# Second layer of a two-stream feed forward: one moving operand of 512 columns in place of two of 256

## The chip, the core and the metric

The kernel runs on one core of a Trainium2 chip. The metric is the device time of one execution in microseconds (us). A core has TensorE (PE, matrix products; PEld are its weight loads), VectorE (DVE), ScalarE (ACT), GpSimd (POOL) and SyncE (SP, which here issues the DMAs). Each engine runs its own instructions in order and waits for the others through semaphores.

## The reference, cut to what matters

The program is a whole small network. Its first block has two layers, and works on two streams of 256 tokens each, `x` (called a below) and `ctx` (called b), both 1024 wide. The second stream ends in the second layer's mixer.

```python
D_MODEL = 1024; SEQ = 256; CTX_LEN = 256; DEPTH = 2; D_FF = 2816
def swiglu(h, w_gate_up, w_down):
    gate, up = jnp.split(h @ w_gate_up, 2, axis=-1)
    return (jax.nn.silu(gate) * up) @ w_down
def sandwich_ffn(x, w_gate_up, w_down, g_pre, g_post, shift, scale, gate):
    h = modulate(rms_norm(x, g_pre), shift, scale)
    return x + 0.5 * gate * rms_norm(swiglu(h, w_gate_up, w_down), g_post)
for l in range(DEPTH):
    x = sandwich_ffn(x, w_ffn_gate_up[l, 0], w_ffn_down[l, 0], ...)
    ctx = sandwich_ffn(ctx, w_ffn_gate_up[l, 0], w_ffn_down[l, 0], ...)
    ... # mixer of both streams
    x = sandwich_ffn(x, w_ffn_gate_up[l, 1], w_ffn_down[l, 1], ...)
    if not last:
        ctx = sandwich_ffn(ctx, w_ffn_gate_up[l, 1], w_ffn_down[l, 1], ...)
```

So three feed forwards of the program have two streams and share their weights between them: layer 0's first and second, and layer 1's first. The change touches `@ w_down` in these three. A second block follows (attention, an mLSTM and two feed forwards of the one stream), which the change does not touch.

## The kernel before

Features lie on the 128 partitions and tokens on the free axis. Every float32 operand of a product is split into a high and a low float32r part, and one term of a product is three matmuls into the same bank of PSUM: high weights by high data, high by low, low by high. ACT makes the high part of a piece of weights (`whi`, L93, 128x1024, eight blocks of 128x128), DVE the low part (`wlo`, L95), from `raw` that SP loads. Six pieces are held at a time (`RING`), three raw ones (`RAW`).

`ffn_two` is the feed forward of two streams. It goes through the hidden width of 2816 in two halves of 11 blocks (`HF`). In each half, for each of the 11 hidden blocks, PE makes the gate and the up product of stream a and then of stream b (`gu`, 258 columns), and `gu_evac` turns each pair into the high and low part of the hidden block: `tg`, `tu` and `af` on DVE, `sl` and `ah` (L250) on ACT, `al` (L251) on DVE. The hidden blocks are kept for each stream apart, in `aha`, `ala`, `ahb`, `alb`.

Then comes the second layer, called "down" here: 8 output blocks of 128 features (`KD`), for each stream, each a sum over the half's 11 hidden blocks. `blocks` issues three matmuls of 256 columns for each term (L597 to L599, tile `ps_dn`), with the depth outermost; output blocks 0 and 1 go on together. `lagged` sets the order of streams and blocks: stream a's blocks 0 and 1, stream b's 0 and 1, then block 2 of a, block 2 of b, and so on. In the second half of the width the last four blocks (`LAG`) are all of a's and then all of b's, so that a's norm can begin while b's blocks run. In the first half ACT copies a finished block out of PSUM (L668); in the second half DVE adds it to that copy (L671), ACT squares it and DVE sums the squares, for the norm behind it (`post`).

PE runs in the order in which the code is written. The order of DVE and ACT is made by the framework's scheduler, with priorities. Beside the products, DVE and the DMA queue work off the modulation vectors: for each of 128 rows `mod_chunk` loads 128x1024 (`wm`) and DVE multiplies it with the conditioning vector (L502). These rows are spread over the three feed forwards by a table (`mods`), some before each down block of stream a.

```python
o = [(a, (0, 1)), (b, (0, 1))]
for d in range(2, KD - lag):
    o += [(a, (d,)), (b, (d,))]
return o + [(a, (d,)) for d in range(KD - lag, KD)] + [(b, (d,)) for d in range(KD - lag, KD)]
```

Of the kernel before, what the change touches and what calls it, by code (L numbers as in the profile page):

```python
# [18 lines left out]
P = 128  # L19
T = 256  # L20
# [17 lines left out]
# columns of the packed parameter array  # L38
# [10 lines left out]
# columns of the packed constants  # L49
# [16 lines left out]
class Stream:  # L66
    """One set of 256 tokens, features on partitions."""


class Weights:  # L70
    """Weights in the order in which they are used: loaded ahead, and split into two float32r parts."""
# [27 lines left out]
    def queued(self):  # L99
        """Long instructions are not to come between the short ones of a norm's chain."""  # L100
        return self.tc.issue_after(self.behind) if self.behind is not None else nullcontext()
# [14 lines left out]
class Chunks:  # L116
    """Weights that come as a row of [128, 128] blocks, eight to a piece."""
# [14 lines left out]
class Kernel:  # L132
    """TensorE runs its instructions in the order written here. Work that waits for other engines is
    held in chains, whose steps are put between the matrix products of the main line."""
# [6 lines left out]
    # ---------------------------------------------------------------- plan of the weights  # L141
# [53 lines left out]
    # ---------------------------------------------------------------- chains  # L195
# [22 lines left out]
    def later(self, c, gap, fn, label=None, after=0):  # L218
        """fn as the next step of a chain: gap terms behind the step before it, after terms from now."""
        c.append([gap, fn, label, self.now + after])  # L220
# [7 lines left out]
    # ---------------------------------------------------------------- small helpers  # L228
# [16 lines left out]
    def split(self, hi, lo, src, scale=None):  # L245
        """hi + lo = src * scale, both float32r."""
# [11 lines left out]
    def mm3(self, out, terms, main=False):  # L258
        """out = sum over terms of (whi + wlo).T @ (xhi + xlo); the product of the low parts is below float32."""
# [9 lines left out]
    def gemm(self, outs, ws, s, n):  # L269
        """Blocks of a product of s's tokens; several blocks go on together, one part of the depth at a time."""  # L270
# [10 lines left out]
    # ---------------------------------------------------------------- norms  # L281
    def rsqrt_v(self, y, v, t):
        """y = v ** -0.5 by Newton's iteration."""
# [10 lines left out]
    def stat(self, s, acc):  # L294
        """s.rt[token] = rsqrt(mean of the squares + eps), tokens on partitions."""
# [14 lines left out]
    def spread(self, s):  # L310
        """s.rt with tokens on the free axis, the same on all partitions."""
# [36 lines left out]
    def begin(self):  # L348
        """The first two modulation vectors, the first norm of both streams, and the first products."""
# [66 lines left out]
    def post(self, s, g5, y, nxt, wait):  # L416
        """x += g5 * rms_norm(y), then the next norm's input: nxt = (factors, shift). y: one tile, or a list
        of blocks."""
# [40 lines left out]
    def residual(self, s, d, ps, nxt, acc):  # L459
        """One block of a product back into the stream, and the next norm's input."""  # L460
# [12 lines left out]
    # ---------------------------------------------------------------- modulation vectors  # L473
    def load_cond(self, pool):
        """silu of the two conditioning vectors, the same on all partitions."""
# [14 lines left out]
    def mod_chunk(self, l, c):  # L490
        """128 entries of a modulation vector, for both streams."""
# [25 lines left out]
    def both(self, l, c):  # L517
        """The second stream ends in the last mixer."""
        return l == 0 or c < 5 * KD

    def mod_done(self, l, vec):
        """Once a vector is there: the factors that norms and residuals take from it."""
# [14 lines left out]
    # ---------------------------------------------------------------- feed forward  # L537
# [16 lines left out]
    def times_r(self, s, t, ps):  # L554
        """Two blocks times r; they lie in one bank of PSUM or in two."""
# [30 lines left out]
    def blocks(self, s, ds, w, n, tag, ready=None):  # L586
        """Blocks ds of a product of depth n * 128, the depth outermost; ready: called before each part."""
# [14 lines left out]

    def lagged(self, streams, lag):
        """Blocks of the last product: the first stream ends some blocks before the second."""
        a, b = streams
        o = [(a, (0, 1)), (b, (0, 1))]
        for d in range(2, KD - lag):
            o += [(a, (d,)), (b, (d,))]
        return o + [(a, (d,)) for d in range(KD - lag, KD)] + [(b, (d,)) for d in range(KD - lag, KD)]

    def ffn_start(self, key, s, n, side=1):
        """The first two products, before the phase's own buffers are there: `side` of them go on together, as
        far as the norm has come."""
# [12 lines left out]
    def ffn_two(self, l, i, first, nxts, start):  # L626
        """Feed forward of two streams, in two halves of the hidden width."""
# [5 lines left out]
        with ExitStack() as es:  # L633
            self.fp = pool = es.enter_context(self.tc.tile_pool(name="ffn", bufs=1))
            for s in self.pair:
                s.ah = pool.tile([P, HF, T], F32R, name="ah" + s.name)
                s.al = pool.tile([P, HF, T], F32R, name="al" + s.name)
# [5 lines left out]
            for h in range(2):  # L643
# [17 lines left out]
                for s, ds in self.lagged(self.pair, LAG if h else 0):  # L661
                    if s is sa:
                        for d in ds:
                            self.mod_chunks(mods.get(KF + h * KD + d, ()))
                    for d, ps in self.blocks(s, ds, lambda d, c: w(HF * d + c), HF, "ps_dn"):
                        y = s.y[:, d, :]
                        if h == 0:
                            nc.scalar.activation(out=y, in_=ps, func=AF.Copy)  # L668
                            continue
# [1053 lines left out]
```

## Time and profile before

| what | value |
|---|---|
| time, median of 3 runs | 2641.85 us (2633.56 to 2644.76) |
| the profiled execution, span from first to last instruction | 2634.0 us |
| PE busy | 2520.9 us, 96% of the span |
| DVE busy | 1858.6 us, 71% |
| ACT busy | 1172.5 us, 45% |
| the six down stretches, from first to last matmul | 59.7, 60.6, 59.7, 60.6, 63.9, 60.6 us |
| matmuls of 256 columns in these | 3168, in six groups of 528 |

For the profiled execution the profile gives only the span; it lies inside the range of the runs, 7.85 us under their median. A busy share counts overlapping instructions once. PE's matmuls are pipelined: a matmul of 256 columns is shown as 0.28 us long, but the next one starts 0.11 us after it, so the pace is read from starts, not from durations. PEclk is the granted clock of TensorE, as a share of 2.4 GHz: 1.00 is 2.4 GHz and 0.50 is 1.2 GHz.

### The profile page before, as it was taken

The numbers are of one execution on the slowest core, as the hardware profiler recorded it, in microseconds if no ns is written. First come the engines' busy times: TensorE is split into PE (matmuls) and PEld (weight loads), VectorE is DVE, ScalarE is ACT, GpSimd is POOL, SyncE is SP. The second block draws the span as 40 slices with busy tenths as digits, with TensorE's granted clock in tenths as the row PEclk, the third lists the DMA queues.
The fourth block names the chain that finished last, engine by engine and source line by source line (L and its number), as shares of the span: only waits on it lengthen the run. The fifth ranks groups of instructions, "written<-read, shape, count | busy, mean of one in ns | idle before, by whom it ended". The sixth has DMA issues, their size and how long they took to land. (4 is left out here: it accounts for less than half of the span.)

```text
span 2634.0 us, 49868 instructions
## 1 busy us (share of the span) xinstructions
PE 2520.9 (96%) x20335; PEld 2445.3 (93%) x20335; DVE 1858.6 (71%) x3734; ACT 1172.5 (45%) x2062; POOL 74.3 (3%) x131
## 2 busy tenths in 40 slices
PE   7999998999999999999999888998999999999998
PEld 5999997889999999999998778998999999978998
DVE  5998548676998546984547767757877676666764
ACT  4332324664432333332334555545555554565442
POOL 0000001210000000000000310000000000000000
PEclk9999998999999999999999989999999999998999
DMA  8666323622566321674232734554444465533553
GB/s 300 206 209 208 106 89 72 80 45 74 183 206 220 104 91 63 221 252 159 97 97 75 88 73 152 194 186 134 152 145 145 133 204 184 168 110 109 189 176 120
DMA packets 105254, 383.17 MB, mean 145 GB/s; under 512 B 13560, under 2 KB 13688, under 8 KB 103360
## 3 DMA queue, kind: packets, MB, share of 16 engines
q1 hardware_dynamic: 101984, 370.89, 42.5%
q0 software_dynamic: 3040, 9.09, 4.3%
q8 instruction: 159, 2.61, 0.4%
q14 instruction: 71, 0.58, 0.1%
HBM read 378.88 MB, written 1.05 MB: 144 GB/s over the span
## 5 line engine op out<-in xcount | busy, mean ns | idle before, releaser
L93 ACT ACTIVATE whi<-raw 128x1024 fp32r<-128x1024 f32 x559 | 588.6, 1055 | 570.9 <-PE gu L277 186.0
L95 DVE TENSOR_TENSOR wlo<-raw,whi 128x1024 fp32r<-128x1024 f32 x559 | 680.4, 1219 | 217.8 <-ACT whi L93 215.7
L278 PE MATMUL gu<-hha,wlo 128*128 128x258 f32 (+1 forms) x2112 | 601.7, 285 | 9.3 <-DVE wlo L95 9.3
L276 PE MATMUL gu<-hha,whi 128*128 128x258 f32 (+1 forms) x2112 | 604.0, 286 | 4.9 <-ACT hha L253 2.9
L277 PE MATMUL gu<-hla,whi 128*128 128x258 f32 (+1 forms) x2112 | 600.6, 284 | 1.4 <-DVE hla L254 1.2
L278 PEld LDWEIGHTS gu<-hha,wlo 128*128 128x128 f32 x2112 | 404.8, 192 | 11.2 <-DVE wlo L95 11.2
L276 PEld LDWEIGHTS gu<-hha,whi 128*128 128x128 f32 x2112 | 403.2, 191 | 6.1 <-ACT hha L253 3.7
L277 PEld LDWEIGHTS gu<-hla,whi 128*128 128x128 f32 x2112 | 404.1, 191 | 2.5 <-DVE hla L254 2.5
L276 PE MATMUL gu<-hhb,whi 128*128 128x258 f32 x1056 | 300.8, 285 | 1.1 <-ACT hhb L253 1.1
L277 PE MATMUL gu<-hlb,whi 128*128 128x258 f32 x1056 | 299.6, 284 | 1.4 <-DVE hlb L254 1.2
L278 PE MATMUL gu<-hhb,wlo 128*128 128x258 f32 x1056 | 297.9, 282 | 0.0
L277 PEld LDWEIGHTS gu<-hlb,whi 128*128 128x128 f32 x1056 | 200.6, 190 | 2.4 <-DVE hlb L254 2.4
L276 PEld LDWEIGHTS gu<-hhb,whi 128*128 128x128 f32 x1056 | 199.3, 189 | 1.5 <-ACT hhb L253 1.5
L278 PEld LDWEIGHTS gu<-hhb,wlo 128*128 128x128 f32 x1056 | 199.7, 189 | 0.0
L502 DVE SCALAR_TENSOR_TENSOR junk<-wm,cond 128x1024 bf16<-128x1024 f32 x128 | 156.5, 1223 | 43.1 <-DMA wm<-w_mod 42.3
L598 PE MATMUL ps_dn<-ala,whi 128*128 128x256 f32 x528 | 146.2, 277 | 2.3 <-DVE ala L251 2.3
L597 PE MATMUL ps_dn<-ah,whi 128*128 128x256 f32 x528 | 147.3, 279 | 0.0
L599 PE MATMUL ps_dn<-ah,wlo 128*128 128x256 f32 x528 | 147.3, 279 | 0.0
L598 PE MATMUL ps_dn<-al,whi 128*128 128x256 f32 x528 | 147.3, 279 | 0.0
L597 PE MATMUL ps_dn<-ahb,whi 128*128 128x256 f32 x528 | 146.8, 278 | 0.0
L598 PE MATMUL ps_dn<-alb,whi 128*128 128x256 f32 x528 | 146.2, 277 | 0.0
L599 PE MATMUL ps_dn<-ahb,wlo 128*128 128x256 f32 x528 | 146.2, 277 | 0.0
(413 smaller groups left out, 6008.1 us busy)
## 6 DMA issues: line engine op xcount, KB each, us to landing
raw<-w_gu SPq DMA_DIRECT2D x176, 512.0 KB, 3.8
wm<-w_mod SPq DMA_DIRECT2D x128, 512.0 KB, 4.3
raw<-w_down SPq DMA_DIRECT2D x88, 512.0 KB, 3.4
raw<-ffn_w_in SPq DMA_DIRECT2D x88, 512.0 KB, 3.5
raw<-attn_w_in SPq DMA_DIRECT2D x72, 512.0 KB, 3.4
raw<-ffn_w_out SPq DMA_DIRECT2D x44, 512.0 KB, 3.4
raw<-w_in SPq DMA_DIRECT2D x32, 512.0 KB, 3.4
raw<-mlstm_w_in SPq DMA_DIRECT2D x24, 512.0 KB, 3.5
```

The costliest lines, as they stand in the source:

```text
L93: nc.scalar.activation(out=hi[:, :n], in_=raw[:, :n], func=AF.Copy)
L95: nc.vector.tensor_tensor(out=lo[:, :n], in0=raw[:, :n], in1=hi[:, :n].bitcast(F32), op=ALU.subtract)
L276: nc.tensor.matmul(o, wh, xh, start=k == 0, stop=False)
L277: nc.tensor.matmul(o, wh, xl, start=False, stop=False)
L278: nc.tensor.matmul(o, wl, xh, start=False, stop=k == KD - 1)
L502: nc.vector.scalar_tensor_tensor(out=out, in0=w, scalar=1.0, in1=self.cond[:, i, :], op0=ALU.mult, op1=ALU.mult, accum_out=m[:, i:i + 1],)
L597: nc.tensor.matmul(o, wh, xh, start=i == 0, stop=False)
L598: nc.tensor.matmul(o, wh, xl, start=False, stop=False)
L599: nc.tensor.matmul(o, wl, xh, start=False, stop=i == n - 1)
```

## The change

`ah` and `al` of both streams become one tile each, `ah2` and `al2`, in which the 256 tokens of a and the 256 of b lie side by side for each hidden block. A new function `blocks_two` (L612 to L614, tile `ps_dn2`) issues three matmuls of 512 columns for each term, for both streams together, into one whole bank of PSUM. It makes all 8 output blocks in the first half of the width, and blocks 0 to 3 in the second half; blocks 4 to 7 of the second half stay as they were, for each stream apart, through `blocks`. A joint block is copied out (or added and squared) in two pieces of 256 columns, right after each other. It calls `tick` twice for each term, as the two streams' terms did.

```diff
+    def blocks_two(self, ds, w, n):
+        nc = self.nc
+        ps = [self.bank("ps_dn2") for _ in ds]
+        for c in range(n):
+            for o, d in zip(ps, ds):
+                wh, wl = w(d, c)
+                xh = self.ah2[:, c].rearrange("p s t -> p (s t)")
+                xl = self.al2[:, c].rearrange("p s t -> p (s t)")
+                nc.tensor.matmul(o, wh, xh, start=c == 0, stop=False)
+                nc.tensor.matmul(o, wh, xl, start=False, stop=False)
+                nc.tensor.matmul(o, wl, xh, start=False, stop=c == n - 1)
+                self.tick()
+                self.tick()
+        return zip(ds, ps)
     def lagged(self, streams, lag):
         a, b = streams
-        o = [(a, (0, 1)), (b, (0, 1))]
-        for d in range(2, KD - lag):
-            o += [(a, (d,)), (b, (d,))]
+        o = [(None, (0, 1))] + [(None, (d,)) for d in range(2, KD - lag)]
         return o + [(a, (d,)) for d in range(KD - lag, KD)] + [(b, (d,)) for d in range(KD - lag, KD)]
...
+            self.ah2 = pool.tile([P, HF, 2, T], F32R, name="ah2")
+            self.al2 = pool.tile([P, HF, 2, T], F32R, name="al2")
             for s in self.pair:
-                s.ah = pool.tile([P, HF, T], F32R, name="ah" + s.name)
-                s.al = pool.tile([P, HF, T], F32R, name="al" + s.name)
+                s.ah, s.al = self.ah2[:, :, s.i], self.al2[:, :, s.i]
...
+                    if s is None:
+                        for d, ps in self.blocks_two(ds, lambda d, c: w(HF * d + c), HF):
+                            for s in self.pair:
+                                y, o = s.y[:, d, :], ps[:, s.i * T:(s.i + 1) * T]
+                                if h == 0:
+                                    nc.scalar.activation(out=y, in_=o, func=AF.Copy)
+                                    continue
+                                with self.tc.high_priority(offset=FIRST):
+                                    nc.vector.tensor_tensor(out=y, in0=o, in1=y, op=ALU.add)
+                                    if d == 0:
+                                        s.acc = self.new_acc(s)
+                                    self.square_into(s.acc, y, d == 0)
+                        continue
```

PE, at the first half's down stretch of the third of these feed forwards (layer 1's first), where the deepest term (the eleventh hidden block) of output blocks 0 and 1 stands. Before, it is stream a's term, and stream b's first term follows. A bracket names the semaphore for which an instruction waits; `Activation_49` and `DVE_49` count the work of ACT and DVE.

```order
L597 MATMUL ps_dn_13984<-aha_12541,whi_13850 128x256 [waits Activation_49]
L598 MATMUL ps_dn_13984<-ala_12542,whi_13850 128x256 [waits DVE_49]
L599 MATMUL ps_dn_13984<-aha_12541,wlo_13851 128x256
L597 MATMUL ps_dn_13985<-aha_12541,whi_13856 128x256
L598 MATMUL ps_dn_13985<-ala_12542,whi_13856 128x256
L599 MATMUL ps_dn_13985<-aha_12541,wlo_13857 128x256
L597 MATMUL ps_dn_14072<-ahb_12544,whi_13724 128x256
L598 MATMUL ps_dn_14072<-alb_12545,whi_13724 128x256
L599 MATMUL ps_dn_14072<-ahb_12544,wlo_13725 128x256
```

The same place after the change:

```order
L612 MATMUL ps_dn2_13162<-ah2_11721,whi_13028 128x512 [waits Activation_49]
L613 MATMUL ps_dn2_13162<-al2_11722,whi_13028 128x512 [waits DVE_49]
L614 MATMUL ps_dn2_13162<-ah2_11721,wlo_13029 128x512
L612 MATMUL ps_dn2_13163<-ah2_11721,whi_13034 128x512
L613 MATMUL ps_dn2_13163<-al2_11722,whi_13034 128x512
L614 MATMUL ps_dn2_13163<-ah2_11721,wlo_13035 128x512
L612 MATMUL ps_dn2_13256<-ah2_11721,whi_13034 128x512
L613 MATMUL ps_dn2_13256<-al2_11722,whi_13034 128x512
L614 MATMUL ps_dn2_13256<-ah2_11721,wlo_13035 128x512
```

The eleventh term now waits for both streams' last hidden block at once, 60 joint matmuls behind the start of the stretch, where before a's term stood 60 matmuls behind the start and b's 66 later; there is no second pass over the terms, and output block 2 follows.

DVE, at the same stretch: what stands ahead of the low part of stream b's eleventh hidden block. `L502` are rows of the modulation vectors, `L95` low parts of weights. Before:

```order
L573 TENSOR_TENSOR tg<-gu,rb 128x258
L502 SCALAR_TENSOR_TENSOR junk,modv_77<-wm,cond 128x1024
L95 TENSOR_TENSOR wlo<-raw,whi 128x1024
L507 TENSOR_TENSOR modv_77<-modv_77,params 128x1
L575 TENSOR_TENSOR tu<-gu,rb 128x258
L502 SCALAR_TENSOR_TENSOR junk,modv_77<-wm,cond 128x1024
L576 SCALAR_TENSOR_TENSOR af<-tu,sl 128x256
L95 TENSOR_TENSOR wlo<-raw,whi 128x1024
L251 TENSOR_TENSOR alb<-af,ahb 128x256
```

and after:

```order
L573 TENSOR_TENSOR tg<-gu,rb 128x258
L502 SCALAR_TENSOR_TENSOR junk,modv_77<-wm,cond 128x1024
L95 TENSOR_TENSOR wlo<-raw,whi 128x1024
L507 TENSOR_TENSOR modv_77<-modv_77,params 128x1
L575 TENSOR_TENSOR tu<-gu,rb 128x258
L502 SCALAR_TENSOR_TENSOR junk,modv_77<-wm,cond 128x1024
L576 SCALAR_TENSOR_TENSOR af<-tu,sl 128x256
L95 TENSOR_TENSOR wlo<-raw,whi 128x1024
L251 TENSOR_TENSOR al_11722<-af,ah_11721 128x256
```

Nothing has moved here: the same two modulation rows and two pieces of weights stand ahead of it. Behind it, pieces of weights stand one or two places earlier among the modulation rows.

## Rows read from the trace of the kernel before

**Rows 1.** The page: span, and PE's busy time, share and instructions.
```profile
span 2634.0 us, 49868 instructions
PE   2520.9 (96%) x20335; PEld 2445.3 (93%) x20335; DVE 1858.6 (71%) x3734; ACT 1172.5 (45%) x2062; POOL 74.3 (3%) x131
```

**Rows 2.** Busy time by stretch: length, engines' busy us (x), PEclk, DMA share, GB/s.
```profile
core 0: us, PE busy (x) PEld busy (x) DVE busy (x) ACT busy (x) POOL busy (x), PEclk, DMA share, GB/s
166.74:226.47 59.73, 59.73 (x530) 59.73 (x528) 54.68 (x101) 18.45 (x30) 0.00 (x0) 1.00 0.73 229
353.52:399.60 46.08, 46.08 (x409) 46.08 (x408) 17.09 (x33) 11.30 (x19) 0.00 (x0) 1.00 0.26 81
1164.36:1228.23 63.87, 61.59 (x529) 61.39 (x528) 37.66 (x67) 19.32 (x32) 0.00 (x0) 0.97 0.64 214
```

**Rows 3.** Timeline of PE, first down stretch: start, length, instruction.
```profile
180.00 0.28 PE L597 MATMUL ps_dn<-ahb,whi 128*128 128x256 f32 x1
...
186.12 0.28 PE L597 MATMUL ps_dn<-ahb,whi 128*128 128x256 f32 x1
```

**Rows 4.** Timeline of PE, fifth down stretch; brackets: idle before and releaser.
```profile
1171.17 0.28 PE L597 MATMUL ps_dn<-aha,whi 128*128 128x256 f32 x1
1173.73 0.58 PE L598 MATMUL ps_dn<-ala,whi 128*128 128x256 f32 x1 [2.28 <-DVE ala L251]
1174.11 0.41 PE L599 MATMUL ps_dn<-aha,wlo 128*128 128x256 f32 x1
...
1174.75 0.41 PE L599 MATMUL ps_dn<-aha,wlo 128*128 128x256 f32 x1
```

**Rows 5.** Busy time by stretch, behind that stall; columns as in rows 2.
```profile
1174.00:1177.10 3.10, 3.10 (x16) 3.10 (x17) 1.62 (x4) 1.46 (x2) 0.00 (x0) 0.50 0.58 182
```

**Rows 6.** Timeline of PE, first mixer: three matmuls of 256, then of 512 columns.
```profile
469.09 0.38 PE L263 MATMUL ps_sc<-kh,qhb 64*128 64x256 f32 x1
469.31 0.28 PE L264 MATMUL ps_sc<-kl,qhb 64*128 64x256 f32 x1
469.44 0.28 PE L265 MATMUL ps_sc<-kh,qlb 64*128 64x256 f32 x1
469.64 0.39 PE L276 MATMUL qkv<-hha,whi 128*128 128x258 f32 x1
...
472.09 0.50 PE L263 MATMUL ps_sc<-kh,qha 64*128 64x512 f32 x1
472.44 0.39 PE L264 MATMUL ps_sc<-kl,qha 64*128 64x512 f32 x1
472.66 0.39 PE L265 MATMUL ps_sc<-kh,qla 64*128 64x512 f32 x1
472.98 0.39 PE L276 MATMUL qkv<-hhb,whi 128*128 128x258 f32 x1
```

**Rows 7.** `ps_dn` on PE by stretch: length, busy (x), PEclk, DMA share, GB/s.
```profile
176.00:226.00 50.00, 50.00 (x443) 1.00 0.74 235
1740.00:1790.00 50.00, 50.00 (x431) 1.00 0.58 190
```

**Rows 8.** Timeline of PE, mLSTM: 8 columns of weights, 256 columns of data.
```profile
2321.91 0.28 PE L1471 MATMUL ps_den<-smh,colr 128*8 128x256 f32 x1
...
2322.38 0.28 PE L276 MATMUL qk<-hha,whi 128*128 128x256 f32 x1
```

**Rows 9.** Timeline of DVE, fifth down stretch.
```profile
1172.10 1.23 DVE L502 SCALAR_TENSOR_TENSOR junk<-wm,cond 128x1024 bf16<-128x1024 f32 x1 [1.91 <-DMA wm<-w_mod]
...
1179.39 0.48 DVE L576 SCALAR_TENSOR_TENSOR af<-tu,sl 128x256 f32<-128x256 f32 x1
1179.79 1.22 DVE L95 TENSOR_TENSOR wlo<-raw,whi 128x1024 fp32r<-128x1024 f32 x1
1180.92 0.42 DVE L251 TENSOR_TENSOR alb<-af,ahb 128x256 fp32r<-128x256 f32 x1
```

**Rows 10.** Timeline of DVE, first down stretch.
```profile
174.74 0.42 DVE L251 TENSOR_TENSOR alb<-af,ahb 128x256 fp32r<-128x256 f32 x1
```

**Rows 11.** Groups of instructions by line: busy, mean ns, idle before and releasers.
```profile
L671 DVE TENSOR_TENSOR ya<-ps_dn,ya 128x256 f32<-128x256 f32 x24 | 9.9, 425 | 48.8 <-PE ps_dn L599 48.8
L668 ACT ACTIVATE ya<-ps_dn 128x256 f32<-128x256 f32 x24 | 9.0, 383 | 42.5 <-PE ps_dn L599 42.5
```

More of the change, by code (lines that the diff above doesn't have):

```diff
@@ L66 @@
 class Stream:
+    pass
 class Weights:
@@ L661, in ffn_two @@
                 for s, ds in self.lagged(self.pair, LAG if h else 0):
-                    if s is sa:
+                    if s is not sb:
                         for d in ds:
                             self.mod_chunks(mods.get(KF + h * KD + d, ()))
+                    if s is None:
[11 more added lines that the diff above has]
+                        continue
                     for d, ps in self.blocks(s, ds, lambda d, c: w(HF * d + c), HF, "ps_dn"):
                         y = s.y[:, d, :]
-                        if h == 0:
-                            nc.scalar.activation(out=y, in_=ps, func=AF.Copy)
-                            continue
                         with self.tc.high_priority(offset=FIRST):
                             nc.vector.tensor_tensor(out=y, in0=ps, in1=y, op=ALU.add)
-                            if d == 0:
-                                s.acc = self.new_acc(s)
-                            self.square_into(s.acc, y, d == 0)
+                            self.square_into(s.acc, y, False)
                         if d == KD - 1:
```

## Prediction

> **What bounds the kernel now.** First the page: PE is busy for 2520.9 of 2634.0 us [rows 1], so the first thing to ask of any stretch is whether PE has a gap in it. Then the busy times of the stretches that the change rewrites. In the first down stretch PE is busy for all of 59.73 us, at the full clock; DVE has 54.68 us of work there, ACT 18.45, the DMA queues 73%. The third is like it. In the second, fourth and sixth (one shown, up to the norm's first transposes) PE is again busy throughout, with DVE and ACT far below. Only the fifth has a gap: 61.59 us busy in 63.87, at a mean clock of 0.97 [rows 2]. So in five of the six stretches the time is PE's pace times a count, and the sixth has one wait in it.
>
> The pace is read from starts. From 180.00 to 186.12 lie 54 matmuls: 6.12 / 54 = 113.3 ns for 256 columns [rows 3]. At 2.4 GHz 256 columns are 106.7 ns, so 6.7 ns of each start-to-start time is something else. At half the clock that piece is gone: from 1174.11 to 1174.75 lie three matmuls, 213 ns each, which is 256 columns at 1.2 GHz [rows 4].
>
> **What the change does to PE.** Matmuls of down: three feed forwards x 11 depths x 3 x (8 + 4 blocks) = 1188 pairs of 256 columns become 1188 matmuls of 512, and 1188 weight loads go. The columns that stream through the array stay the same. So all that can be won on PE is that 6.7 ns, and the question is whether it belongs to the instruction (then a joint matmul takes 220.0 ns against 226.7 for the pair) or to the columns (then 226.7, and nothing is won).
>
> The weight loads themselves are no answer: with 8 columns of weights in place of 128, four matmuls of 256 columns take from 2321.91 to 2322.38, 117 ns each [rows 8]. A load a sixteenth as wide leaves the pace where it was, so the loads lie beside the stream, and their removal is costed at nothing; the cover is the stream of the matmul before, which gets longer.
>
> No float32r matmul over 128 rows and 512 columns is in this trace; the nearest rows have 64 rows of contraction. There three matmuls of 256 columns, up to the next instruction, take 469.64 - 469.09 = 0.55 us, and three of 512 take 472.98 - 472.09 = 0.89 [rows 6]. The 256 more columns cost 0.34 / 3 = 113 ns each. At one column per cycle they would cost 106.7, three of them 0.32 us. The change of row groups at both ends is the same in both and drops out. So here the extra time grows with the columns, and I take 226.7 ns: **0 us**. I keep 220.0 as the low bound: 1188 x 6.7 = 8 us less. For the high bound I take the slowest pace that the same kind of matmul shows elsewhere: in the one-stream feed forward 50 us hold 431 where the two-stream one has 443 [rows 7], 113.3 x 443 / 431 = 116.5 ns, with nothing different but where the operand lies. At that pace a joint matmul takes 233, 1188 x 6.3 = 7.5 us more.
>
> A page speaks for the low side. The Trainium skill, "TensorE: Matmul & The Clock Gate", section "Back-to-back issue gap", gives a warm gap of N / 2.4 + 2.5 ns, a fixed cost per matmul. By it 512 columns would take 215.8 ns, and 1188 x (226.7 - 215.8) = 13 us would be won. This trace does not agree with it at 256 columns: the page gives 109.2, the rows 113.3.
>
> **The other engines.** A block is read out of PSUM by as many instructions of the same size as before (383 and 425 ns each); ACT and DVE waited 42.5 and 48.8 us for PE there, not the other way round [rows 11]. They now come in pairs, behind the joint block; the next block goes into another bank of the eight, so PE does not wait for them. The last four blocks of the second half, and with them the norm behind, keep their order: 0 us. Pieces of weights are wanted at the same mean rate. Inside the first two blocks they are wanted later than before (the first block of the third piece stood 33 matmuls in, 3.7 us; now 33 joint ones, 7.5 us) and let go earlier, so no new wait for weights; modulation rows keep their count. 0 us.
>
> **The one wait.** In the fifth stretch a's eleventh term starts at 1171.17, and its second matmul finds `al` unfinished until 1173.73 [rows 4]: 1173.73 - 1171.28 = 2.45 us lost. The whole stretch is 63.87 - 59.73 = 4.14 longer than the first [rows 2], so 1.7 us more are left: behind the wait 3.1 us hold 16 matmuls at a clock of 0.50 [rows 5], each about 100 ns longer, which is 1.6. The joint pass asks for this term at 1164.36 + 60 x 0.2267 = 1177.96, some 7 us later, so the wait for a goes. But it asks for b's at the same moment. b's `al` comes at 1180.92 + 0.42 = 1181.34 [rows 9]; before, nobody wanted it until 66 matmuls after a's term. DVE's order in front of it has not moved, and what it stands behind is not PE: DVE was idle 1.91 us for a modulation row's DMA [rows 9]. So the wait takes the place of the one removed: the joint second matmul would start at 1178.19 and starts at 1181.4, 3.2 us lost, and the clock falls again, 1.7. That is 4.9 against 4.1: **+0.8 us**. If DVE had run through earlier, all of it could go: bound -4.1. The other starts are safe: the latest b comes at 174.74 + 0.42 - 166.74 = 8.4 us into the first stretch [rows 10], and is asked for at 13.6. That cover of 5.2 us is worth some 5 us a stretch if it is ever gone.
>
> **Sum.** 0 + 0 + 0.8: a span of 2634.8 against 2634.0. The median shown lies 7.85 above this execution; carried over, 2642.6 us.
>
> **Rivals.**
> 1. The 6.7 ns belong to the instruction. For it: the piece is gone at half the clock, as an issue cost beside a longer stream would be (but so would be a supply of columns that is only too slow for the full clock). Against it: the triples of rows 6, 0.34 and not 0.32 us. Joint matmuls at 220.0: -8.0 + 0.8, and + 0.4 because the wait is met 60 x 6.7 ns earlier: about 2635 us. If the joint one cost its columns alone, 213.3 ns, it would be 2627. The skill's page named above states a rule of this form; by its figure the time would be 2630.
> 2. The slower side: the stream of 2 KB per partition is fetched at the slower of the two paces of rows 7. For it: the pace does depend on where the operand lies, and nothing in the trace shows why. Against it: the new tiles replace the old ones in the same pool, and blocks start 2 KB apart as in the mixer's rows. 233 ns, +7.5 + 0.8: 2650 us. It is over 0.5% slower only from a joint pace of 226.7 + (13.2 - 0.8) / 1188 = 237 ns on.
> 3. The wait is gone: DVE's order around it is as before, but the queue in front of the DMAs is not PE's to move, and pieces of weights behind it stand earlier. If b's last block comes 3.4 us sooner, 2642.6 - 4.9 = 2638.
> 4. That the change saves nothing where it means to, since it streams the same columns, is the forecast itself.
>
> **How the numbers follow.** Chances: forecast 0.60; rival 1 0.24; rival 2 0.08; rival 3 0.08. The forecast alone has its own width from the scatter of the runs, 2637 to 2647. Half a per cent is 13.2 us, about what a measurement of this kernel can tell from no change. Rival 1 at 220.0 stays inside that, at 213.3 it does not, so I give a third of it, 0.08, to faster, and 0.03 for a wait removed that I have not seen: 0.11. Slower needs a pace over 237 or waits in two or three more stretches: 0.08. The rest, 0.81, is within. The range of 8 in 10 takes in rival 1 at 220.0 less 5 us of scatter, rival 3, and rival 2: 2630 to 2650.
>
> **What would show it.** In the profile after: starts of `ps_dn2` 0.227 us apart (0.220 for rival 1, 0.233 for rival 2); the first down stretch 59.7 us long again (57.9 for rival 1); in the fifth stretch an idle of some 3 us before L612 and L613 at the eleventh term, released by b's `ah` and `al`, and the clock at 0.50 behind it; no wait of PE in the other five; ACT and DVE groups of the copies with the same counts. The forecast is wrong if the joint pace is off 226.7 by more than 10 ns, or if a second stretch waits.

## The result, and the profile after

| | median | lowest to highest | runs |
|---|---|---|---|
| before | 2640.96 us | 2633.56 to 2644.76 | 4 |
| after | 2653.30 us | 2648.96 to 2656.44 | 4 |

The ratio is 1.0057, 95% interval 1.0039 to 1.0075. (The ratios here are those of the record; they are not the quotients of the two medians, which here is 1.0047.) Between the medians the changed kernel is slower by 12.3 us, where +0.8 was forecast. The changed kernel was timed once more, beside its own runs of before: 2645.66 us against 2638.59, ratio 1.0033 (1.0017 to 1.0050). So it is slower both times, by 7 to 12 us between the medians.

The page of the changed kernel, to be read beside [rows 1]:

```profile
span 2647.2 us, 47498 instructions
...
PE 2532.6 (96%) x19147; PEld 2401.6 (91%) x19147; DVE 1853.7 (70%) x3734; ACT 1168.6 (44%) x2062; POOL 75.1 (3%) x131
```

PE has 1188 matmuls less and is busy for 11.7 us more. (In the second execution, below, it is 6.8 more, so a part of this is scatter.) The columns that stream through are as many as before, so somewhere they seem to have become dearer. Next the first, second and fifth down stretch, as in [rows 2] (the second here in its full length):

```profile
core 0: us, PE busy (x) PEld busy (x) DVE busy (x) ACT busy (x) POOL busy (x), PEclk, DMA share, GB/s
167.63:228.99 61.36, 61.36 (x265) 49.19 (x264) 55.03 (x101) 17.73 (x29) 0.00 (x0) 1.00 0.71 228
356.19:417.70 61.51, 61.29 (x402) 55.02 (x401) 29.67 (x68) 20.18 (x35) 0.00 (x0) 1.00 0.30 86
1169.38:1233.53 64.15, 61.90 (x266) 49.31 (x265) 38.04 (x69) 18.71 (x31) 0.00 (x0) 1.00 0.67 222
```

The first is 61.36 us long, was 59.73, and PE is busy in all of it at the full clock: no wait has come in. The six stretches were 59.73, 60.57, 59.73, 60.56, 63.87, 60.57 and are 61.36, 61.51, 61.36, 61.50, 64.15, 61.50. That is 6.35 us in all. Where all eight blocks are joint the loss is 1.63, where four are it is 0.94, about half. So the loss goes with the joint matmuls, and the pace shows it. PE's timeline in the first stretch, for [rows 3] (the profile leaves out numbers at the end of a name, so `ps_dn2` stands as `ps_dn`, and `ah2` as `ah`):

```profile
179.76 0.39 PE L613 MATMUL ps_dn<-al,whi 128*128 128x512 f32 x1
...
186.06 0.39 PE L613 MATMUL ps_dn<-al,whi 128*128 128x512 f32 x1
```

Between these starts lie 27 matmuls: 6.30 / 27 = 233.3 ns for 512 columns, 560 cycles at 2.4 GHz, where the pair took 226.7. Then the wait in the fifth stretch, PE and DVE, for [rows 4, 9]:

```profile
1183.14 0.40 PE L614 MATMUL ps_dn<-ah,wlo 128*128 128x512 f32 x1
1185.26 0.49 PE L612 MATMUL ps_dn<-ah,whi 128*128 128x512 f32 x1 [1.72 <-ACT ah L250]
1186.28 0.51 PE L613 MATMUL ps_dn<-al,whi 128*128 128x512 f32 x1 [0.53 <-DVE al L251]
```
```profile
1178.16 1.23 DVE L502 SCALAR_TENSOR_TENSOR junk<-wm,cond 128x1024 bf16<-128x1024 f32 x1 [2.42 <-DMA wm<-w_mod]
...
1183.12 1.23 DVE L502 SCALAR_TENSOR_TENSOR junk<-wm,cond 128x1024 bf16<-128x1024 f32 x1 [0.30 <-DMA wm<-w_mod]
...
1185.81 0.42 DVE L251 TENSOR_TENSOR al<-af,ah 128x256 fp32r<-128x256 f32 x1
```

It sits where it was forecast, at the eleventh hidden block, and is released by stream b's `ah` and `al`. DVE, which makes that `al`, had stood idle for 2.42 us, up to 1178.16, for a modulation row's DMA, and later for 0.30 more. The stretch is 64.15 - 61.36 = 2.8 us longer than the first; before, it was 4.1. The clock does not fall behind it this time.

The other 6.9 us of the 13.2 between the two spans lie outside the six stretches, in parts that differ both ways: the first mixer's is 2.8 us shorter, the second mixer's with the first products behind it 4.3 longer, the mLSTM's 2.7 longer. Behind the third two-stream feed forward the order of DVE, ACT and POOL is the same in both kernels, so no change of order made the last two. Whether they come back is asked below.

### The profile page after: what moved, and what is told of

It is laid out like the page before. It is cut to its first block, busy times and chain, and to the rows that moved or that the text cites. A ratio compares the mean times of both kernels' runs of the same rounds, so it can differ in the third digit from the quotient of the medians.

```text
span 2647.2 us, 47498 instructions
## 1 busy us (share of the span) xinstructions
PE 2532.6 (96%) x19147; PEld 2401.6 (91%) x19147; DVE 1853.7 (70%) x3734; ACT 1168.6 (44%) x2062; POOL 75.1 (3%) x131
## 5 line engine op out<-in xcount | busy, mean ns | idle before, releaser
L95 DVE TENSOR_TENSOR wlo<-raw,whi 128x1024 fp32r<-128x1024 f32 x559 | 679.6, 1217 | 239.2 <-ACT whi L93 237.3
L597 PE MATMUL ps_dn<-ah,whi 128*128 128x256 f32 x792 | 220.8, 279 | 0.0
L598 PE MATMUL ps_dn<-al,whi 128*128 128x256 f32 x792 | 220.2, 278 | 0.0
L599 PE MATMUL ps_dn<-ah,wlo 128*128 128x256 f32 x792 | 220.2, 278 | 0.0
L250 ACT ACTIVATE ah<-af 128x256 fp32r<-128x256 f32 x198 | 82.0, 416 | 301.6 <-DVE af L576 250.6
L502 DVE SCALAR_TENSOR_TENSOR junk<-wm,cond 128x1024 bf16<-128x1024 f32 x128 | 156.4, 1222 | 45.2 <-DMA wm<-w_mod 44.0
L612 PE MATMUL ps_dn<-ah,whi 128*128 128x512 f32 x396 | 156.2, 394 | 1.7 <-ACT ah L250 1.7
L613 PE MATMUL ps_dn<-al,whi 128*128 128x512 f32 x396 | 156.2, 395 | 0.5 <-DVE al L251 0.5
L614 PE MATMUL ps_dn<-ah,wlo 128*128 128x512 f32 x396 | 156.1, 394 | 0.0
```

What stands on the lines that cost most here:

```text
L95: nc.vector.tensor_tensor(out=lo[:, :n], in0=raw[:, :n], in1=hi[:, :n].bitcast(F32), op=ALU.subtract)
L502: nc.vector.scalar_tensor_tensor(out=out, in0=w, scalar=1.0, in1=self.cond[:, i, :], op0=ALU.mult, op1=ALU.mult, accum_out=m[:, i:i + 1],)
L597: nc.tensor.matmul(o, wh, xh, start=i == 0, stop=False)
L598: nc.tensor.matmul(o, wh, xl, start=False, stop=False)
L599: nc.tensor.matmul(o, wl, xh, start=False, stop=i == n - 1)
L612: nc.tensor.matmul(o, wh, xh, start=c == 0, stop=False)
```

## The experiments

**The joint matmul cut in two, with all else as changed.**

```diff
-                nc.tensor.matmul(o, wh, xh, start=c == 0, stop=False)
...
+                for a, b in ((0, T), (T, 2 * T)):
+                    nc.tensor.matmul(o[:, a:b], wh, xh[:, a:b], start=c == 0 and a == 0, stop=False)
+                    nc.tensor.matmul(o[:, a:b], wh, xl[:, a:b], start=False, stop=False)
+                    nc.tensor.matmul(o[:, a:b], wl, xh[:, a:b], start=False, stop=c == n - 1 and b == 2 * T)
```

> The changed kernel with each joint matmul of 512 columns cut into two of 256 from the same two tiles, into the same bank, in the same order of output blocks. Theory (length): the 233.4 ns of a joint matmul belong to one operand of 512 columns; cut in two it costs 113.3 ns each again, the first down stretch is 59.7 us long and not 61.4, and the time is some 7.9 us below the changed kernel's, 2645. Rival (place): the joint bank or the order of blocks costs it; then each half stays at 116.7 ns, the stretch at 61.4 us and the time at 2653. Of the 13.2 us between the two profiles 6.4 lie in the six down stretches and 6.9 outside. If these 6.9 are scatter between executions and no work of the change, this kernel takes what the kernel before takes, 2641 +- 4; if the order of the blocks makes them, it takes 2645 to 2648.

Measured: 2637.03 us against 2638.93, ratio 1.0001 (0.9983 to 1.0019). First and fifth stretch:

```profile
167.01:226.74 59.73, 59.73 (x529) 59.73 (x528) 54.14 (x103) 17.72 (x29) 0.00 (x0) 1.00 0.68 230
1165.62:1228.83 63.21, 60.29 (x530) 59.89 (x528) 38.67 (x69) 18.61 (x31) 0.00 (x0) 1.00 0.68 225
```

59.73 us to the hundredth, from the same tiles, into the same bank, in the same order of blocks. Tiles, banks and order cost nothing on PE; the loss goes with one instruction of 512 columns, or with its one weight load in place of two, which a later run sets apart. The wait stays with the order (63.21), and is no reason for the difference.

**Joint in the first half of the width alone.**

```diff
+        if lag:
+            o = [(a, (0, 1)), (b, (0, 1))]
+            for d in range(2, KD - lag):
+                o += [(a, (d,)), (b, (d,))]
```

> The joint matmuls in the first half of the hidden width alone; the second half's eight output blocks for each stream apart, in the order of before. Length theory: 792 joint matmuls x 6.7 ns = 5.3 us over the kernel before, 2646; first, third and fifth down stretch 61.4 us (the fifth with its wait 64.1), second, fourth and sixth 60.6 again. If the loss were a single event of one of the second halves, this kernel would be at 2641; if it were the joint wait in the fifth stretch, at 2653.

Measured: 2644.66 us, ratio 1.0021 (1.0010 to 1.0032), 5.7 us over before. Its first two stretches:

```profile
166.99:228.35 61.36, 61.36 (x265) 49.19 (x264) 53.68 (x99) 17.85 (x29) 0.00 (x0) 1.00 0.73 226
355.54:416.10 60.56, 60.43 (x533) 60.24 (x532) 30.27 (x68) 20.39 (x35) 0.00 (x0) 1.00 0.28 88
```

Two thirds of the joint matmuls should bring two thirds of 1188 x 6.7 = 7.9 us, which is 5.3; the 5.7 agrees with it, and the halves without them are back at 60.56.

**The changed kernel again.**

> The changed kernel again, unaltered, for the part of the difference that lies outside the six down stretches (6.9 us of 13.2 between the two profiles). If only the pace of the joint matmuls and the two waits belong to the change, the down stretches sum to 6.4 us more again, the rest of the span falls within the 2269 to 2276 us that the profiles so far show, and the median is 6 to 9 us over the kernel before, ratio 1.0025 to 1.0035. If the change makes waits elsewhere too, the ratio is 1.0047 or more again.

Measured: ratio 1.0033, as the first of the two theories has it. The joint stretches without a wait are 61.36 and 61.51 us again. The rest of the span is 2268.2 us, where the first profile of this kernel had 2275.8 and before 2269.0; in the profiles of the pairs, of the first half alone and of the 16-byte step (below) it is 2270.2, 2271.7 and 2272.7. So one kernel's rest differs by 7.6 us between two executions. The second mixer's part is 0.9 us longer than before's here and the mLSTM's 2.3 shorter, where they were 4.3 and 2.7 longer: the 6.9 us did not come back, and are not shown to belong to the change. A few us outside the stretches are not excluded by this; the two rows (below) have a rest of 2277.0. The wait, though, is longer, and the clock falls behind it:

```profile
1183.40 0.40 PE L614 MATMUL ps_dn<-ah,wlo 128*128 128x512 f32 x1
1186.72 0.80 PE L612 MATMUL ps_dn<-ah,whi 128*128 128x512 f32 x1 [2.93 <-ACT ah L250]
1187.74 0.79 PE L613 MATMUL ps_dn<-al,whi 128*128 128x512 f32 x1 [0.23 <-DVE al L251]
...
1169.64:1237.24 67.60, 64.45 (x265) 51.10 (x264) 39.59 (x71) 18.60 (x31) 0.00 (x0) 0.95 0.66 214
1188.40:1192.60 4.20, 4.20 (x11) 3.24 (x10) 2.05 (x6) 2.15 (x5) 0.00 (x0) 0.50 0.92 312
```

The stretch is 67.60 - 61.36 = 6.2 us over one without a wait, 2.1 more than before's 4.1; in the first profile it was 1.4 less. In other runs with the same order around it, it goes from 0.3 us (the 16-byte step, below) to 6.3 (the two rows, below, with the clock's mean at 0.95 again):

```profile
1170.50:1238.19 67.69, 64.59 (x265) 51.06 (x264) 39.39 (x71) 19.48 (x32) 0.00 (x0) 0.95 0.65 218
```

The order of DVE around that `al` is the same in all of these. What differs is when DVE gets the modulation row: 6.3 us into the stretch with the 16-byte step, 8 to 10 in the first-half, changed, repeated, paired, shifted and two-row kernels; in each of these seven profiles `al` is done 7.8 to 8.1 us after that. So the row's DMA sets the wait, and one execution's wait is no measure of the next one's.

**Where the operand starts.** Two kernels move the joint tiles. The first puts 16 bytes between one hidden block and the next, the second starts both tiles 32, 64 and 96 bytes further on in the three feed forwards.

```diff
+            self.ah2 = pool.tile([P, HF, 2 * T + 4], F32R, name="ah2")
+            self.al2 = pool.tile([P, HF, 2 * T + 4], F32R, name="al2")
```

> The changed kernel with 16 bytes between one hidden block of the joint tiles and the next, so that the start of the operand goes through four places within 64 bytes as the hidden block goes from 0 to 10. Length theory: 233 ns at all four places. Rival (address): the pace repeats in fours of the hidden block and differs by 3 ns or more between the places, as the one-stream feed forward's 116.7 ns against 113.3 do between tiles that start 32 bytes apart; the place with the lowest pace tells whether 226.7 or 220 can be had.

```diff
+            at = 8 * (1 + i + 2 * l)
+            ah2 = pool.tile([P, HF * 2 * T + 32], F32R, name="ah2")
+            al2 = pool.tile([P, HF * 2 * T + 32], F32R, name="al2")
+            self.ah2 = ah2[:, at:at + HF * 2 * T].rearrange("p (c s t) -> p c s t", s=2, t=T)
+            self.al2 = al2[:, at:at + HF * 2 * T].rearrange("p (c s t) -> p c s t", s=2, t=T)
```

> The changed kernel with both joint tiles read from 32, 64 and 96 bytes further on, in the first, second and third two-stream feed forward: the operand starts at 64, 96 and 0 bytes past a multiple of 128, where it started at 32. If 560 cycles for 512 columns are the supply's steady pace: 233 ns at every place. If the place matters as for 256 columns: another pace in each of the three, and the blocks of 256 columns in the second halves (113.3 ns at 32) go to 116.7 at 0; a place with 227 ns or less would win the 7.9 us back.

Measured with the 16 bytes, first and fifth stretch:

```profile
166.61:227.41 60.80, 60.80 (x266) 49.41 (x265) 53.65 (x99) 17.86 (x29) 0.00 (x0) 1.00 0.70 227
1168.60:1229.70 61.10, 61.07 (x266) 49.34 (x264) 35.74 (x64) 18.18 (x30) 0.00 (x0) 1.00 0.69 222
```

That is 231 ns for each matmul. Single ones go from 225 to 241 ns, and the means of the four places are 231.0, 231.2, 231.3 and 231.4: the pace does not go by the place. With the shifted tiles, the first stretch of each feed forward (by the layout, starts at 64, 96 and 0 past a multiple of 128):

```profile
166.91:227.69 60.78, 60.78 (x266) 49.40 (x265) 56.28 (x104) 17.84 (x29) 0.00 (x0) 1.00 0.74 237
785.64:847.00 61.36, 61.36 (x266) 49.45 (x264) 54.62 (x100) 17.02 (x28) 0.00 (x0) 1.00 0.70 227
1171.96:1236.44 64.48, 61.88 (x266) 49.38 (x264) 38.82 (x69) 18.71 (x31) 0.00 (x0) 1.00 0.66 221
```

263 steps in 60.78 us are 231.1 ns, in 61.36 233.3 (the third has the wait in it). No place comes near 226.7, and the blocks of 256 columns lose their 113.3: without the few steps over 130 ns, they take 117.1, 117.9 and 118.4 ns in the three second halves. There a pair costs 234 to 237 ns, and the joint matmul beside it, at 231 to 233, is the cheaper one.

**The one-stream tiles 32 bytes further on, in the kernel before.**

```diff
+            ah = pool.tile([P, KF * T + 32], F32R, name="ah")
+            s.ah = ah[:, 8:8 + KF * T].rearrange("p (c t) -> p c t", t=T)
```

> The kernel before, with the two tiles of the hidden width in the one-stream feed forward read from 32 bytes further on (their start was a multiple of 128 bytes, that of the two-stream ones is 32 more than one). Place theory: where the operand starts within 128 bytes decides between 116.7 and 113.3 ns for 256 columns; then the three one-stream down stretches (first to last start) go from 61.5 to 59.7 us and the time falls by 5.3 us, to 2635 where before stands at 2640. Rival (something else of the one-stream form, such as its depth of 22 blocks): 61.5 us and no change.

Measured: 2639.21 us, ratio 1.0005 (0.9992 to 1.0018). The place theory fails, and so does its rival: the one-stream stretches, 61.49, 61.48 and 61.48 us before, get longer, 61.68, 62.07 and 62.07.

```profile
1732.63:1794.31 61.68, 61.68 (x529) 61.68 (x528) 27.83 (x29) 27.62 (x37) 0.00 (x0) 1.00 0.54 180
```

**Two rows of 256 columns in place of one of 512.**

```diff
+            self.ah2 = pool.tile([P, 2, HF, T], F32R, name="ah2")
...
+                xh = self.ah2[:, :, c]
```

> The changed kernel with the tiles laid out as before, all of stream a's hidden blocks and then all of b's, so that a joint operand is two rows of 256 columns 11,264 bytes apart. If the columns of one instruction set its pace: 233 ns and the same stretches as the changed kernel's (61.4 us). If a long row does: 227 ns or 220, stretches of 59.7 or 57.9 us, and a version with joint matmuls that takes no more than the kernel before.

Measured: the first stretch is 61.36 us, and `ps_dn` holds 216 matmuls in 50 us, as in the changed kernel. So it is not the length of a row in memory that sets the pace; the number of columns of the instruction is what all the slow ones share.

```profile
170.00:220.00 50.00, 50.00 (x216) 1.00 0.69 227
```

**A ladder of cuts.**

```diff
+CUTS = {
+    0: (0, 512), 1: (0, 512), 2: (0, 256, 512), 3: (0, 128, 256, 384, 512), 4: (0, 384, 512),
+    5: (0, 192, 384, 512), 6: (0, 448, 512), 7: (0, 320, 512),
+}
```

> The changed kernel with the 512 columns cut differently for each output block of the first half: 512 (blocks 0 and 1), 2 x 256, 4 x 128, 384 + 128, 192 + 192 + 128, 448 + 64, 320 + 192. Length theory, through the two points 256 columns = 272 cycles and 512 = 560: 1.125 cycles per column less 16 for each matmul, so 384 columns take 173.3 ns, 320 143.3, 192 83.3, 128 53.3, 448 203.3. Rival (a fixed cost of 16 cycles for each matmul and something else at 512): 384 take 166.7 ns, 320 140.0, 192 86.7, 128 60.0, 448 193.3. Rival (a step at a length over 256): 384 and 320 lie on neither line. The short ones may be held up by their weight loads; then 128 and 64 columns take the same.

PE's timeline, output blocks 3 and 4:

```profile
200.16 0.28 PE L619 MATMUL ps_dn<-al,whi 128*128 128x128 f32 x1
...
200.82 0.28 PE L619 MATMUL ps_dn<-al,whi 128*128 128x128 f32 x1
...
207.54 0.34 PE L619 MATMUL ps_dn<-al,whi 128*128 128x384 f32 x1
207.72 0.34 PE L620 MATMUL ps_dn<-ah,wlo 128*128 128x384 f32 x1
207.89 0.22 PE L618 MATMUL ps_dn<-ah,whi 128*128 128x128 f32 x1
207.95 0.27 PE L619 MATMUL ps_dn<-al,whi 128*128 128x128 f32 x1
208.06 0.28 PE L620 MATMUL ps_dn<-ah,wlo 128*128 128x128 f32 x1
```

Six matmuls of 128 columns take 0.66 us, 110 ns each: nearly as much as 256 columns. Right behind a long one the first short one is through in 0.06 us, and the next takes 0.11 again. So something other than the stream seems to hold the short ones to 108 to 114 ns, and to be done ahead of time behind a long matmul. The long ones, means over 66 steps each, without the first of each three, which stands behind that floor: 320 columns 146.3 ns, 384 174.8, 448 204.4, 512 233.3. Per column that is 0.457, 0.455, 0.456 and 0.456 ns, 35/32 of a cycle. The line of the expectation, 1.125 cycles per column less 16 (143.3, 173.3, 203.3), is too low by 1 to 3 ns, and the rival of a fixed cost (140.0, 166.7, 193.3) by 6 to 11.

**Fewer columns of weights.**

```diff
+CUTS = {
+    0: (128, WHOLE), 1: (128, WHOLE), 2: (64, WHOLE), 3: (8, WHOLE),
+    4: (64, PAIR), 5: (8, PAIR), 6: (128, PAIR), 7: (8, FOUR),
+}
```

> The changed kernel with fewer columns of weights in hidden blocks 1 to 9 of the first half, which leaves out the rest of these output features: joint with 128 columns (output blocks 0, 1), 64 (2), 8 (3); two matmuls of 256 with 64 (4), 8 (5), 128 (6); four of 128 with 8 (7). If the load of the weights sets the floor of 112 ns that matmuls of 128 and 192 columns showed, four of 128 columns with 8 columns of weights go to some 58 ns each. If the load disturbs the stream of a matmul, the joint ones fall from 233 ns with 64 and 8 columns, towards 213. If the load has no part in it: 233 ns, 113 ns and still 112 ns for 128 columns.

```profile
222.49 0.22 PE L621 MATMUL ps_dn<-al,whi 128*8 128x128 f32 x1
...
223.15 0.22 PE L620 MATMUL ps_dn<-ah,whi 128*8 128x128 f32 x1
```
```profile
194.92 0.40 PE L622 MATMUL ps_dn<-ah,wlo 128*8 128x512 f32 x1
...
195.62 0.40 PE L622 MATMUL ps_dn<-ah,wlo 128*8 128x512 f32 x1
```

With 8 columns of weights, 128 columns of data take 0.66 / 11 = 60.0 ns: the floor was the load. Three joint ones with 8 columns of weights still take 0.70 us, 233 ns each. The load has no part in the joint pace. The Trainium skill, "TensorE: Matmul & The Clock Gate", section "LDWEIGHTS (loading the stationary operand)", gives P / 1.2 ns for P columns of weights, 106.7 for 128; the floor of 108 to 114 ns agrees with it.

**Rows, neighbours, repeated data.**

```diff
+KINDS = "joint", "joint", "rows64", "pairs64", "turns", "mixed", "same", "twice"
...
+                parts = {"pairs64": (two,) * 3, "turns": (two if c % 2 else one,) * 3, "mixed": (one, two, one)}
```

> The changed kernel with another kind of matmul in hidden blocks 1 to 9 of each output block of the first half: joint (output blocks 0, 1), joint and pairs with 64 of the 128 rows (2, 3; the other rows are left out), joint on every other hidden block with pairs between (4), the middle one of the three a pair (5), the high part of the data in place of the low one (6), stream a's 256 columns twice in place of a's and b's (7). Theory (columns of one instruction): above 256 columns a matmul takes 35/32 cycles per column, whatever is next to it: 233 ns for every joint one, 113 for every half of a pair. Rival (sustained run): the joint ones are slow only one after another; between pairs (4, 5) they take 227 ns or less. Rival (rows): the three 64-row matmuls in the first mixer, 113 to 115 ns for 256 columns more, are a property of 64 rows; then output block 2 takes 227. Rival (fetch): the 2 KB of a row that is fetched without a break cost it; then 256 columns twice take 227 or less.

```profile
187.71 0.39 PE L626 MATMUL ps_dn<-ah,wlo 64*128 64x512 f32 x1
187.94 0.40 PE L626 MATMUL ps_dn<-ah,whi 64*128 64x512 f32 x1
188.17 0.39 PE L626 MATMUL ps_dn<-al,whi 64*128 64x512 f32 x1
188.41 0.40 PE L626 MATMUL ps_dn<-ah,wlo 64*128 64x512 f32 x1
```

Three of 64 rows take 0.70 us: 233 ns, in the same shape that [rows 6] priced at 227. Pairs of 64 rows stay at 113 to 114. The same data twice has a mean of 233 ns, and so has the high part in place of the low one. Between pairs the joint ones take 225 to 236 ns, mean 231; eight of 18 are at 227 or less, but the halves of the pairs beside them take 113 to 122, mean 116. Two joint ones and the pair between them come to 693 to 700 ns, and 2 x 233.3 + 226.7 is 693.3: nothing is won. So the rivals of rows and of the fetch fail, and that of the sustained run fails on the sum.

**A little over 256 columns.**

```diff
+CUTS = {d: (0, n, 512) for d, n in enumerate((512, 512, 258, 264, 272, 288, 304, 256))}
```

> The changed kernel with the 512 columns of the first half cut a little beyond the middle: 258 + 254 (output block 2), 264 + 248 (3), 272 + 240 (4), 288 + 224 (5), 304 + 208 (6), 256 + 256 (7); blocks 0 and 1 joint. It asks where the 272 cycles for 256 columns end and the 35/32 cycles per column of 320 to 512 begin. Gradual: 258 take 114 ns, 272 take 120 (272 + 16 cycles), 288 take 127 and 304 take 133; one cycle per column more. Step at 256: 258 take 118 to 120 ns at once, as the gate and up products of 258 columns do, 272 take 124, 288 take 131, 304 take 139 (35/32 cycles per column). The short second parts take 112 to 113 ns, the floor of a weight load, either way.

```profile
184.35 0.28 PE L616 MATMUL ps_dn<-ah,whi 128*128 128x258 f32 x1
...
185.79 0.28 PE L616 MATMUL ps_dn<-ah,whi 128*128 128x258 f32 x1
...
194.97 0.28 PE L618 MATMUL ps_dn<-ah,wlo 128*128 128x248 f32 x1
195.09 0.29 PE L616 MATMUL ps_dn<-ah,whi 128*128 128x264 f32 x1
...
196.51 0.29 PE L616 MATMUL ps_dn<-ah,whi 128*128 128x264 f32 x1
```

Six matmuls of 258 and six of 254 columns, between the first two lines, take 1.44 us, and six of 264 and six of 248, between the last two, 1.42; twelve of 256 take 1.36 where the pace is 113.3. The medians of the three matmuls of 258 columns are 116, 121 and 119 ns; without the first of each three, 272 take 124 and 288 132 to 135. The gradual line (114, 120, 127) is too low for all of them, so two columns over 256 are enough. But the 254 columns beside the 258 take 120 to 124 too: they are under 256, and start 1032 bytes into the row and not 1024. So this run does not part a step in the length from what the uneven cut does to the neighbour.

**Three output blocks going on together, with pairs.**

```diff
-        o = [(None, (0, 1))] + [(None, (d,)) for d in range(2, KD - lag)]
+        o = [(None, (0, 1, 2))] + [(None, (d,)) for d in range(3, KD - lag)]
```

> The kernel of the pairs (two matmuls of 256 columns in the joint order) with output blocks 0, 1 and 2 going on together in place of 0 and 1, so that the eleventh hidden block is asked for 90 x 0.2267 = 20.4 us into the stretch and not 13.6. In the fifth down stretch stream b's last low part came 17 us after the start. If the wait there is all that keeps the stretch above 59.8 us, it goes: 59.8 in place of 63.2, and the time falls to some 2635 where before stands at 2639. Rival: pieces of weights are then asked for sooner than they are ready (the third block's first piece stands 6 matmuls in), and waits for them come in the first halves; the stretches get longer.

Measured: 2632.55 us against 2640.44, ratio 0.9983 (0.9969 to 0.9997). It is the one version here whose interval lies below the kernel before. The fifth stretch is 62.29 us, not 59.8:

```profile
1195.70 0.28 PE L614 MATMUL ps_dn<-al,whi 128*128 128x256 f32 x1
1198.26 0.38 PE L615 MATMUL ps_dn<-ah,wlo 128*128 128x256 f32 x1 [2.29 <-DVE wlo L95]
```
```profile
1193.29 1.23 DVE L502 SCALAR_TENSOR_TENSOR junk<-wm,cond 128x1024 bf16<-128x1024 f32 x1 [1.86 <-DMA wm<-w_mod]
1194.44 0.08 DVE L502 DVE_READ_ACCUMULATOR junk<-wm,cond 128x1 f32 x1
1194.56 0.16 DVE L507 TENSOR_TENSOR modv<-modv,params 128x1 f32<-128x1 f32 x1
1195.63 1.22 DVE L502 SCALAR_TENSOR_TENSOR junk<-wm,cond 128x1024 bf16<-128x1024 f32 x1 [0.91 <-DMA wm<-w_mod]
...
1196.98 1.23 DVE L95 TENSOR_TENSOR wlo<-raw,whi 128x1024 fp32r<-128x1024 f32 x1
```

The wait for `al` is gone, and one for a piece of weights, as the rival had it, stands in its place, 33 us into the stretch. Its cause is the same: DVE stands idle for a modulation row's DMA, with the piece queued behind it. Of the 0.17%, some 4 us, the profile shows 63.87 - 62.29 = 1.6 in this stretch, but two of the second halves are 0.5 us longer than before, so that the six together are 0.6 shorter. I do not assign the rest, which is inside the scatter outside the stretches, and the win is not shown to come from the order.

## Why the prediction was wrong, point by point

- **What bounds the stretches** was right: PE's pace times a count in five of six, one wait in the sixth.
- **The joint matmul, "the extra time grows with the columns, and I take 226.7 ns: 0 us"**, is the step that failed. It takes 233.3, so the term is 1188 x 6.7 = +7.9 us, and with it the sum would be +8.7, between the two measured 7.1 and 12.3. The question behind it, whether the 6.7 ns belong to the instruction or to the columns, had no room for columns that are dearer in a longer instruction. The pairs show that nothing else of the change costs anything on PE. What misled me is the 64-row triple. The 28 undisturbed triples of 512 columns in the two mixers have a median of 892 ns against 547 for 256, 115 ns for 256 columns more, so [rows 6] are no outlier; but in an unbroken run the same 64-row shape takes 233, which is 120 more. The price was read from 0.34 us where the unbroken run makes 0.36, two units of the timeline's last digit. Three matmuls between others are no steady pace. Why the triples look cheaper was not tried.
- **The rule of the page that spoke for the low side**, the Trainium skill, "TensorE: Matmul & The Clock Gate", "Back-to-back issue gap", N / 2.4 + 2.5, which it calls the gap of an isolated matmul, does not hold here: 55.8, 109.2 and 215.8 ns for 128, 256 and 512 columns would win 13 us; the rows show 60.0, 113.3 and 233.3.
- **Rival 1, a cost of the instruction**, holds up to 256 columns: 60.0 ns are 128 + 16 cycles, 113.3 are 256 + 16. It does not hold at 512, which would be 220.0.
- **Rival 2** had the price, 233: the measured 233.3 is twice the 116.7 of the one-stream feed forward, the slower of the paces that it named. That the joint one falls to it because of where it lies is not borne out: where the operand starts moves the joint pace between 231 and 233 ns only, and two rows of 256 columns leave it alone. Whether one cause is behind both is open.
- **The weight loads at nothing**: the forecast holds, but a little closer than I had it. A load takes 108 to 114 ns, a matmul of 256 columns 113.3; they lie beside the stream with almost nothing to spare, and the matmuls of 128 and 192 columns in the ladder were no faster (110 to 112 ns).
- **The one wait, +0.8**: the mechanism was right. Its size was -1.4 in one execution and +2.1 in another, with the clock at 0.50 behind the longer one. It hangs on when a modulation row lands, which differs by 3.7 us between profiles with the same order, so one trace could not give it to a us.
- **The other engines, 0**: the blocks are read out by as many instructions (ACT twice 24, DVE four times 12), and PE waited in no other stretch, but for 0.2 us at the norm's first transposes in each second half.
- **The range** ended at rival 2's own sum and left out the scatter above it, while 5 us were taken off below. The rest of the span of one and the same kernel came out as 2268.2 and 2275.8 us.

Still open: why 256 columns in an unbroken run from the two-stream tiles take 272 cycles (113.3 ns), and about 280 (116.7) or more from the one-stream tiles, from every shifted tile, often beside a joint matmul, and with 64 columns of weights (mean 119 ns; with 8 it is 113 again). For 256 columns 280 cycles are 35/32 of a cycle per column, as in the long ones, so it may be the 113.3 that is the exception. The shifts show that the start within 128 bytes alone does not decide it.

## What to carry to other kernels

Fewer and longer matmuls save nothing by themselves on a PE that is busy throughout: with float32r operands and these tiles 256 columns were the best length, and cutting a joint matmul of 512 back into two halves won the whole loss back. This hangs on the 113.3 ns: from the shifted tiles two of 256 took 234 to 237 ns and one of 512 231 to 233, so measure both at the place where the operand lies. Take the price of a matmul from an unbroken run of the same shape, and if there is none, let the range reach to the dearest pace that the trace shows, with the scatter of the runs on top. A wait behind an engine that runs in order can move to the next thing queued there, as it did with three blocks going on together; look for what that engine itself waits for.

## What the runs showed of the hardware that I had not expected

- A float32r matmul of 320 to 512 columns took 35/32 of a cycle per column at a granted clock of 1.00: 146.3, 174.8, 204.4 and 233.3 ns for 320, 384, 448 and 512 (231 for 512 from two of the shifted layouts). Up to 256 columns it can take the columns and 16 cycles: 60.0 ns for 128 (with 8 columns of weights) and 113.3 for 256. At 258 columns the medians are already 116 to 121 ns.
- The gate and up products of this kernel have 258 columns, and are as dear as the 258 of the last cuts: between the first and the second down stretch of the changed kernel 1056 of them take 126.96 us, 120.2 ns each. What they would take with 256 was not tried.
- Loading 128 columns of weights holds a run of short matmuls to 108 to 114 ns each (60.0 with 8 columns), and behind a long matmul the first short one is through in 0.06 us, as if one load were done ahead.
